# A two-layer token mixer on eight cores: pooling as running sums on VectorE with one grouped projection, a reordered opening, a wide value projection and a new pacing of background work

## The chip, the cores and the metric

The program runs on the 8 cores of one Trainium2 chip; each core takes one sequence of the batch of 8. The time is the device time of the slowest core, in microseconds (us), and a kernel's figure is the median of its runs. A core's *span* is the time from its first to its last instruction, and the *granted clock* is the share of TensorE's full speed that the hardware allows it at that time. Cores 0 to 3 are one die of the chip, 4 to 7 the other. A run can fall into a slower state, in which some cores show a lower granted clock than the others. Only runs outside that state are compared here, unless it is said.

Names in the profile: PE is TensorE, PEld its weight loads, DVE is VectorE, ACT is ScalarE, POOL is GpSimd, SP is SyncE. "ps" is a PSUM bank (the memory that TensorE writes its results to; all other tiles named here lie in SBUF, the main memory on the core), H the normalised input of a sub-layer, ACTB the SwiGLU products, X the residual stream, SLOTS the weights, WMOD the modulation rows, CB the conditioning vector (and later a pooling buffer), SQ and SP the squares and their pair sums (this SP is a tile and not the engine), RS the reciprocal root mean squares, TP temporaries, PMH the pooling input. All operations are issued through one helper, so every line carries the same number (L323 before, L331 after); they are told apart by tiles.

## The reference, cut to what matters

```python
for l in range(2):
    mod_f1, mod_mx, mod_f2 = split(silu(c) @ w_mod[l] + b_mod[l], 3)   # shift, scale, gate each
    x = x + 0.5 * gate * swiglu(modulate(x, mod_f1), w_ffn_in[l, 0], w_ffn_out[l, 0])
    x = x + gate * (mixer_ab(h) if l % 2 == 0 else mixer_pool(h))
    x = x + 0.5 * gate * swiglu(modulate(x, mod_f2), w_ffn_in[l, 1], w_ffn_out[l, 1])
return rmsnorm(x, final_g)
# modulate(x) = rmsnorm(x) * g * (1 + scale) + shift

def mixer_pool(h, w_grp, scale):            # layer 1 only
    cum = jnp.cumsum(h, axis=1)
    for i, w in enumerate((2, 4, 8, 16)):   # four groups of 256 channels
        prev = shift cum by w tokens
        p = (cum - prev) / minimum(t + 1, w) - h     # trailing mean minus the token itself
        outs.append(p @ w_grp[i])
    return concatenate(outs) * scale
```

The width is 1024, a sequence has 2048 tokens, and the SwiGLU's hidden width is 2816.

## The kernel before

The kernel keeps the 2048 tokens of a core as four tiles of 512 and treats them in two passes, p0 and p1, of two tiles. Each SwiGLU of each pass is a gate/up stage and a down stage for a first group of hidden columns, then the same for a second group. Everything that isn't a large matmul (the squares and sums for the next normalisation, the pooling, the modulation rows) is *background work*. The program is scheduled at build time: a generator yields steps, and after each segment of four to sixteen large matmuls `pump` may issue one.

```python
def pump(n=1, rows=True):
    for _ in range(n):
        if bg and bg_state[0] <= Sd.tl["pe"].tail():
            bg_step()                      # one step of the first generator in bg
    if rows:
        rows_pump()

def rows_pump():                           # ROW_EVERY = 7
    row_tick[0] += 1
    if row_tick[0] % ROW_EVERY == 0:
        ...                                # dot product of one modulation row, on VectorE

def square_pair(c, t):                     # one step of the statistics
    qs = [sq_rot.next(), sq_rot.next()]
    for i, q in enumerate(qs):
        act(SQ[:, q, :], Xv(c + i, t), AF.Square, ...)
    z = sp_rot.next()
    op = add("pool", I("tensor_tensor", out=SP[:, z, :], in0=SQ[:, qs[0], :], in1=SQ[:, qs[1], :], op=ALU.add), ...)
    return z, op.end + 0.3                 # summed over channels later by a matmul with ONES
```

The pooling is a background generator too. It projects first and applies the window afterwards, as a product with a banded 128x128 matrix. TensorE does both (cut):

```python
def pm_gen(p):
    for i in range(4):                                     # window w = 2 ** (i + 1)
        ... # VectorE and ScalarE: PMH = modulated input of two channel chunks, two tiles
        for n2 in range(4):                                # projection, 256 columns
            for k in range(2):
                for kc in range(2):
                    mm(PS[bk][:, k * 256:(k + 1) * 256], PMH[...tokens...], PMW[...], ..., n=256)
            act(GTv[...], PS[bk][:], AF.Copy, ...)
        for dd in range(2):
            for tt in range(2):
                for n in range(4):                         # band, 128 columns
                    mm(PS[bk][:, n * 128:(n + 1) * 128], GTv[...], BANDv[i], ..., n=128)
                    mm(PS[bk][:, n * 128:(n + 1) * 128], prev, BPREVv[i], ..., n=128)
                stt(Xv(dch, t), PS[bk][:], GH[...], Xv(dch, t), ALU.mult, ALU.add, ...)
```

It runs beside the second half of layer 1's first SwiGLU for p0, and beside the first pass of its second SwiGLU for p1. I call these two stretches (down of group 0, then gate/up of group 1) the *pooling windows*.

Two more parts matter. The opening loads x first, then the modulation rows. And at three boundaries between stages the reciprocal root of the statistics (Ln and Exp on ScalarE) is put ahead of the last gate/up segments (the prediction calls it rstd):

```python
side = build_h(nxt) if last and nxt is not None else iter(())
if last and late_norm:
    rstd(other, after=Sd.tl["pe"].tail())
run_segs([first[0], tail3[0], tail3[1], first[1], tail3[2], first[2]], side)
```

## Time and profile before

| | before |
|---|---|
| time | 2031.86 us, median of 4 runs (2030.88 to 2032.13) |
| profiled run, cores 0, 1, 4 to 7 | spans of 2027.4 to 2030.1 us, mean granted clock 0.979 to 0.995 |
| profiled run, cores 2 and 3 | 2057.0 and 2055.4 us, clock 0.965 and 0.966 |

In the profiled run, cores 2 and 3 were disturbed. So I read the other cores, mostly core 5. The page itself is of the slowest core, 2. These are its line of busy times and the first line of its chain of work that ended last.

```profile
PE 1994.9 (97%) x9458; PEld 934.6 (45%) x9458; DVE 1463.5 (71%) x2848; ACT 928.2 (45%) x1523; POOL 328.9 (16%) x431
...
PE 90%; DVE 5%; ACT 2%; DMA 1%; POOL 1%; issue 0%; SPq 0%; DVEq 0%; POOLq 0%
```

TensorE is busy for 97% of the span and makes up 90% of the chain. The list of TensorE's waits on core 5, from 62 us to the end, has the columns total, number and longest; these are its main lines.

```profile
PE ps L323 <- DVE ACTB L323: 9.6, 4, 3.0
PE ps L323 <- POOL SP L323: 3.6, 2, 2.7
PE ps L323 <- DVE X L323: 3.1, 3, 1.4
PE ps L323 <- DVE ps L323: 2.7, 5, 0.9
```

Three of the four waits on ACTB, 2.9 to 3.0 us each, are the three boundaries shown in code above. In the timeline one of them is the bracket at the end of this line (start, duration, then the wait of 3.01 us before it):

```profile
1535.52 14.81 PE L323 MATMUL ps<-ACTB,SLOTS 128*128 128x512 f16 x62 [3.01 <-DVE ACTB L323]
```

The groups of TensorE that belong to the value projection (first line) and to the pooling (the other two: projection, then band) are these, on core 5: count, busy time, mean ns, and idle time before them.

```profile
L323 PE MATMUL ps<-SLOTS,H 128*128 128x256 f16 x256 | 30.6, 273 | 0.0
L323 PE MATMUL ps<-WMOD 128*128 128x256 f16 x128 | 19.2, 273 | 0.0
L323 PE MATMUL ps<-PMC,WMOD 128*128 128x128 f16 x240 | 19.1, 219 | 0.0
```

The busy time overlaps between pipelined matmuls, so it overstates: the 256-column ones last 273 ns each but start 109 ns apart. What a matmul delays the next is read from the starts: 0.2153 us for 512 columns (0.2158 in the mean of all dense stretches of core 5). VectorE was idle for 19 us in the opening, waiting for the first modulation row (list of VectorE's waits, 0 to 80 us):

```profile
DVE ACTB L323 <- DMA ACTB<-wmod: 18.9, 1, 18.9
```

For the comparison I cut each core's trace at fixed counts of weight matmuls. That gives a ledger: the duration of each stage, the sum of TensorE's waits in it, and its *work* (columns / 2400 + 0.0026 us per matmul, a fit to the starts of dense matmuls in before: 0.2158, 0.1092 and 0.0558 us apart for 512, 256 and 128 columns; it fits dense stretches within 0.1 us). What remains I call the *remainder*. On core 5 of before it is 26.0 us. Of this, 16.5 us are the end of the program after the last matmul, some 5 us are three stretches of 3.41 us at a granted clock of 0.5 behind the boundary waits, and some 3 us lie in the first stage, which runs at 0.5 up to 67.0 us. The rest is gaps too short to count as waits.

### The profile page before, as it was taken

How to read it: one execution, taken by the hardware profiler on the slowest of the kernel's cores; microseconds unless marked ns; L12 is line 12 of the kernel's file. 1: busy time of each engine (PE TensorE's matmuls, PEld its weight loads, DVE VectorE, ACT ScalarE, POOL GpSimd, SP SyncE). 2: the span in 40 equal slices, each digit the busy share in tenths (PEclk: the TensorE clock that was granted, in tenths of full speed). 3: DMA queues.
4: the chain of work that ended last, by engine and by line, in shares of the span. 5: the costliest groups of instructions: out<-in, count | busy, mean ns of one | idle time of the engine just before them, and what ended most of it. 6: DMA issues, size and time to landing. Idle time of an engine off the chain costs nothing.

```text
span 2057.0 us, 26258 instructions; the slowest of 8 cores (2027.4 to 2057.0 us)
## 1 busy us (share of the span) xinstructions
PE 1994.9 (97%) x9458; PEld 934.6 (45%) x9458; DVE 1463.5 (71%) x2848; ACT 928.2 (45%) x1523; POOL 328.9 (16%) x431
## 2 busy tenths in 40 slices
PE   5899999999999899999999999999999999999996
PEld 4444444445454344444444444444544445444442
DVE  4876897777787967697779855865775547675654
ACT  4433644254353541554155524554673435744242
POOL 3102030014040200120002100110122001220001
PEclk5899999999999999999999999999998889999998
DMA  9795868675666566667766654445343442446652
GB/s 279 169 242 118 173 136 178 144 151 114 140 108 142 93 124 146 125 139 156 160 135 145 134 97 79 78 85 90 57 80 57 77 69 52 82 65 110 140 85 82
DMA packets 71390, 248.77 MB, mean 121 GB/s; under 512 B 7136, under 2 KB 7264, under 8 KB 70752
## 3 DMA queue, kind: packets, MB, share of 16 engines
q0 software_dynamic: 46928, 153.63, 45.9%
q1 hardware_dynamic: 24336, 93.45, 13.7%
q8 instruction: 79, 1.29, 0.2%
q14 instruction: 47, 0.39, 0.1%
HBM read 392.29 MB, written 8.39 MB: 195 GB/s over the span
## 4 chain that ended last, share of the span: by engine, by line
PE 90%; DVE 5%; ACT 2%; DMA 1%; POOL 1%; issue 0%; SPq 0%; DVEq 0%; POOLq 0%
PE ps L323 90%; DVE X L323 1%; DVE TP L323 1%; DVE SLOTS L323 1%; DMA WMOD<-wmod 1%; POOL SP L323 1%; DMA X<-xT 1%; DVE ACTB L323 1%; DVE H L323 1%; ACT H L323 1%; ACT L323 0%; DVE WMOD L323 0%; ACT RS L323 0%; POOL STAT L323 0%; DVE STAT L323 0%
## 5 line engine op out<-in xcount | busy, mean ns | idle before, releaser
L323 PE MATMUL ps<-H,SLOTS 128*128 128x512 f16 x5440 | 1226.3, 383 | 6.2 <-DVE ps L323 2.4
L323 PEld LDWEIGHTS ps<-H,SLOTS 128*128 128x128 f16 x5440 | 534.4, 99 | 652.6 <-issue 67.6
L323 PE MATMUL ps<-ACTB,SLOTS 128*128 128x512 f16 x3072 | 695.3, 386 | 12.0 <-DVE ACTB L323 8.9
L323 ACT ACTIVATE ps<-ps 128x512 f32<-128x512 f32 x528 | 307.2, 582 | 599.6 <-PE ps L323 586.2
L323 PEld LDWEIGHTS ps<-ACTB,SLOTS 128*128 128x128 f16 x3072 | 303.7, 99 | 384.1 <-issue 57.7
L323 DVE SCALAR_TENSOR_TENSOR X<-ps,GH,X 128x512 f32<-128x512 f32 x320 | 233.1, 747 | 151.0 <-PE ps L323 150.0
L323 DVE TENSOR_TENSOR ACTB<-TP,ps 128x512 f16<-128x512 f32 x368 | 251.5, 687 | 108.9 <-PE ps L323 71.4
L323 ACT ACTIVATE TP<-ps 128x512 f32<-128x512 f32 x400 | 238.7, 597 | 176.9 <-PE ps L323 174.5
L323 DVE TENSOR_TENSOR SLOTS<-SLOTS 128x512 f16<-128x512 f16 x704 | 310.2, 460 | 9.8 <-DMA SLOTS<-win 0.4
L323 DVE TENSOR_TENSOR TP<-ps,TP 128x512 f32<-128x512 f32 x176 | 121.6, 691 | 209.4 <-ACT ps L323 208.8
L323 POOL DMA_DIRECT2D SLOTS<-win x176 | 95.3, 541 | 1023.7 <-PE ps L323 997.3
L323 ACT ACTIVATE SQ<-X 128x512 f32<-128x512 f32 x224 | 134.3, 624 | 213.7 <-DVE X L323 142.5
L323 POOL TENSOR_TENSOR SP<-SQ 128x512 bf16<-128x512 f32 x112 | 153.3, 1373 | 195.7 <-ACT SQ L323 193.9
L323 DVE SCALAR_TENSOR_TENSOR WMOD<-WMOD,CB 128x512 f32<-128x512 f32 (+1 forms) x259 | 175.5, 708 | 3.2 <-DMA WMOD<-wmod 3.1
L323 DVE TENSOR_TENSOR ps<-ps,TP 128x512 f32<-128x512 f32 x176 | 122.9, 698 | 35.6 <-PE ps L323 35.3
L323 ACT ACTIVATE H<-TP,MODT,AS 128x512 f16<-128x512 f32 x160 | 121.3, 805 | 48.8 <-DVE TP L323 41.4
L323 DVE TENSOR_TENSOR TP<-X,RS 128x512 f32<-128x512 f32 x192 | 129.9, 714 | 6.3 <-ACT RS L323 3.9
L323 POOL DMA_DIRECT2D SLOTS<-wout x64 | 45.5, 710 | 336.3 <-PE ps L323 336.3
L323 PE MATMUL ps<-SP,ONES 128*128 128x512 bf16 x122 | 49.3, 416 | 26.4 <-POOL SP L323 22.2
L323 DVE TENSOR_TENSOR H<-H 128x1024 f16<-128x1024 f16 (+1 forms) x72 | 43.7, 628 | 2.9 <-ACT H L323 1.9
L323 ACT ACT_TABLE_LOAD x29 | 37.2, 1283 | 1.5 <-PEq L329 1.1
L323 POOL DMA_DIRECT2D SLOTS<-wab x28 | 15.9, 568 | 128.0 <-PE ps L323 127.6
(76 smaller groups left out, 493.9 us busy)
## 6 DMA issues: line engine op xcount, KB each, us to landing
SLOTS<-win POOLq DMA_DIRECT2D x176, 512.0 KB, 5.5
WMOD<-wmod SPq DMA_DIRECT2D x134, 512.0 KB, 6.1
SLOTS<-wout POOLq DMA_DIRECT2D x32, 768.0 KB, 8.8
SLOTS<-wout POOLq DMA_DIRECT2D x32, 640.0 KB, 6.9
SLOTS<-wab POOLq DMA_DIRECT2D x28, 512.0 KB, 7.5
X<-xT SPq DMA_DIRECT2D x4, 2048.0 KB, 17.3
outT<-X SPq DMA_DIRECT2D x16, 512.0 KB, 4.6
ACTB<-wmod SPq DMA_DIRECT2D x10, 512.0 KB, 19.9
```

The costliest lines, as they stand in the source:

```text
L323: return lambda E: getattr(E, name)(*a, **k)
```

## The change

The intent is to take work off the bounding engine. The window sum of pooling becomes a running sum over tokens on VectorE (add the token that enters, subtract the one that leaves), and TensorE only multiplies the result by the grouped weights, in 512-column matmuls. The extra VectorE work is to be spread by a pacing that looks at how far VectorE is behind in the build-time schedule. The statistics at the three boundaries are finished later, the opening loads modulation rows before x and shares them between TensorE and VectorE, and the value projection uses 512 columns. The diff, cut to its core:

```diff
+    def slack():
+        return Sd.tl["dve"].busy_after(Sd.tl["pe"].tail() - 0.5) < SLACK      # SLACK = 2.0 us
+
     def pump(n=1, rows=True):
-        for _ in range(n):
-            if bg and bg_state[0] <= Sd.tl["pe"].tail():
+        for _ in range(2 * n):
+            if bg and bg_state[0] <= Sd.tl["pe"].tail() and slack():
                 bg_step()
@@ rows_pump
-        if row_tick[0] % ROW_EVERY == 0:
+        if row_tick[0] >= ROW_EVERY and slack():
+            row_tick[0] -= ROW_EVERY
@@ v_stats: one 512-column matmul per channel chunk, was two of 256
@@ pm_gen (the band matrices of pm_consts and the projection of 256 columns are gone)
+   add("dve", I("tensor_tensor_scan", sv, PMH[:, c, cols], PMH[:, c, 16 - w + tt * TT:16 - w + (tt + 1) * TT],
+                init, ALU.add, ALU.subtract), ...)
+   add("dve", I("tensor_copy", SLAST[:, ch:ch + 1], PMS[:, (tt + 1) * TT - 1:(tt + 1) * TT]), ...)
+   op = stt(out, PMH[:, c, cols], -float(w), sv, ALU.mult, ALU.add, ...)   # w = 2: one subtraction instead
...
+                    for kc in range(2):
+                        mm(PS[bk][:], PMW[...], PMD[:, kc, tt * TT:(tt + 1) * TT], kc == 0, kc == 1, ...)
@@ opening
-    x loaded ahead of nine rows; squares in pairs; each chunk's shift row on PE, scale row on VectorE
+    six rows loaded, then x, then three rows; nine of the sixteen rows on PE; squares straight to bf16 in SP
@@ phase loop
-                if last and late_norm:
-                    rstd(other, after=Sd.tl["pe"].tail())
-                run_segs([first[0], ...], side)
+                late = last and late_norm
+                run_segs([first[0], ...], iter(()) if late else side)
+                if late:
+                    rstd(other, after=Sd.tl["act"].tail())
```

## The prediction

> **What bounds the kernel now.** TensorE. The page gives PE 97% of the span and 90% of the chain that ended last. On undisturbed core 0 (2027.4 us) the list of waits gives PE only about 23 us of waits after 60 us. The timeline shows dense 512-column matmuls at 0.2153 us each, so only PE columns, PE waits and the opening can pay. VectorE is busy 71%, but more where the background work runs.
>
> **Pooling, PE side (gain, certain).** Timeline of core 0, 1410-1500 and 1650-1730 us: a projection bank (4 matmuls of 256) delays PE by 0.44 us, a band bank (8 of 128) by 0.445. Removed: 128 x 0.109 + 248 x 0.056 = 27.8 us. Added: 64 matmuls of 512 x 0.2153 = 13.8 us. Net -14 us.
>
> **Pooling, VectorE side (cost).** Added per pass: 12 scans, 12 multiply-adds (about 0.73 us), 4 fp16 subtractions (0.42). [...] In the windows where it must fit (1412.6-1517 and 1643.5-1748 us) VectorE is busy 75 and 72 us of 104.4. [...] the statistics that follow (before: 1501-1512 us, paced by GpSimd) must still end before the drain. I expect PE waits of about 5 us per pass (0 to 12), +10 us together.
>
> **Late rstd.** Three boundaries (250, 1534, 1765 us) each have a 3.0 us PE wait on the SwiGLU product, because ScalarE runs Ln/Exp and its table loads ahead of the gate evacuations. Deferring it removes 9 us, but the next h is then built in about 28 us of down projection that already hold about 30 us of VectorE work. Net -4 us.
>
> **Opening.** Steady matmuls start at 61.9 us. VectorE idles 19 us waiting for the first modulation row behind x, then limits: 4.5 to 4.9 us busy per 5 us from 40 to 65 us. Three of its eight rows (1.5 us each) move into that idle time, one moves to PE, and about 2.5 us of pooling-constant work leaves. Against it, x lands some 10 us later (3.1 MB at about 315 GB/s). From my sum, first sustained matmuls at 55-58 us: -5 us.
>
> **Value projection.** 16 x 256 columns take 1.75 us per block, 8 x 512 should take 1.73: -0.3 us. Weight loads halve, but they are hidden. Pacing of rows by VectorE backlog: -1 us.
>
> **Sum:** -14 + 10 - 4 - 5 - 1 = about -14 us; allowing for what I may have missed, 2018 us. Range 2003 to 2034. Faster by over 2%: 0.03; within 2%: 0.95; slower by over 2%: 0.02.
>
> **What would show each step.** Pooling PE: no 256- or 128-column pooling matmuls, 64 of 512, PE busy down by some 14 us. VectorE: [...] VectorE over 90% in the two pooling windows, and new PE waits on VectorE or GpSimd near their ends; if they are under 1 us, my cost is wrong. Late rstd: the 3.0 us waits gone, with new waits on X or ps just after. Opening: VectorE's 19 us wait gone, sustained matmuls by 58 us. Value: same time per block.
>
> **What would make it wrong.** [...] If the drains serialise VectorE, PE, ScalarE and GpSimd, both passes lose over 10 us and the gain vanishes. If row loads and casting weight loads collide in the opening, its gain turns negative.

For matmuls see the starts above. Weight loads of 99 ns overlap them: from 60 to 1900 us of core 0 PE is busy 1818 us and PEld 847. Ahead of boundary 2 on core 5, ScalarE runs a table load (1.28 us), Ln and Exp (1.33 and 1.13) from 1523.0 us and another table load (1.28) at 1530.4; VectorE waits 1.70 us for the evacuation behind that, and TensorE 3.01 us for VectorE's product. In the opening the DMA moved 272 to 354 GB/s on core 0 (10 to 35 us).

## The result

| | before | after |
|---|---|---|
| median (range), 4 runs each, same chip | 2031.86 (2030.88 to 2032.13) | 2040.84 (2037.8 to 2041.15) |
| ratio of fast runs | 1 | 1.0042, 95% interval 1.0024 to 1.0059 |
| profiled cores, undisturbed | 2027.4 to 2030.1 | 2031.8 to 2035.5 |

A ratio is the mean time of one kernel's fast runs over that of the other's fast runs of the same rounds, so it is not quite the ratio of the medians. The change is within 2%, but it made the kernel 0.4% slower, and the time lies above the predicted range of 2003 to 2034. All runs are correct.

The page of after (its slowest core, 0), busy line and chain:

```profile
PE 1964.4 (97%) x9042; PEld 897.8 (44%) x9042; DVE 1513.6 (74%) x2874; ACT 911.8 (45%) x1503; POOL 313.4 (15%) x410
...
PE 80%; DVE 15%; DMA 2%; ACT 1%; issue 1%; POOL 0%; SPq 0%; DVEq 0%; POOLq 0%
```

VectorE's share of the chain rose from 5% to 15%. TensorE lost the work it was meant to lose. These are the groups of core 5 that replace those shown of before:

```profile
L331 PE MATMUL ps<-SLOTS,H 128*128 128x512 f16 x128 | 28.3, 379 | 0.0
L331 PE MATMUL ps<-CB,WMOD 128*128 128x512 f16 x64 | 18.2, 379 | 0.0
```

The ledger of core 5 gives TensorE's work as 1919.7 us before and 1905.3 after: 14.4 us less. But its waits grew from 22.3 to 37.7 us, and the remainder from 26.0 to 29.2. The list of waits of core 5 tells which kind grew:

```profile
PE ps L331 <- DVE ps L331: 19.9, 14, 2.9
PE ps L331 <- DVE X L331: 7.7, 7, 1.7
PE ps L331 <- POOL SP L331: 4.9, 4, 2.7
...
PE ps L331 <- DVE ACTB L331: 0.8, 1, 0.8
```

The 3.0 us waits on ACTB are gone; one of 0.8 us is left. Waits for GpSimd (SP) grew little. In their place come 14 waits for VectorE operations in PSUM ("DVE ps") of up to 2.9 us, and 7 on X. Where they lie, from the ledger (median over the undisturbed cores):

| stage (us) | before | after |
|---|---|---|
| opening + first gate/up | 58.94 + 78.21 | 59.36 + 75.52 |
| boundary 1, down | 38.70 | 36.33 |
| gate/up after it | 75.12 | 77.16 |
| layer 0, SwiGLU 2, first gate/up of p0 and of p1 | 77.43 and 76.32 | 78.49 and 77.35 |
| layer 1, SwiGLU 1, p0: first gate/up | 74.25 | 79.76 |
| pooling window 1 (down + gate/up) | 44.86 + 72.42 | 44.03 + 73.85 |
| boundary 2, down; gate/up after it | 39.34; 74.25 | 35.71; 76.78 |
| pooling window 2 (down + gate/up) | 44.97 + 72.76 | 44.03 + 72.54 |
| boundary 3, down; gate/up after it | 39.38; 74.25 | 34.78; 80.55 |

The pooling windows came out even. They took 235.0 us before and 234.5 after, although TensorE has 14 us less to do in them: it waits 6.0 and 4.9 us there, and 1.2 to 1.3 us more in each are remainder. That is short gaps around the waits, not a lower clock: the granted clock is 1.00. This is the gate/up stage of window 1 on core 5, before and after. The columns are window, length, then busy time and count for PE, PEld, DVE, ACT and POOL, then granted clock, DMA share and GB/s.

```profile
1454.10:1526.50 72.40, 72.40 (x427) 37.93 (x426) 50.73 (x90) 52.44 (x91) 15.45 (x17) 1.00 0.45 76
```

```profile
1456.30:1530.10 73.80, 67.76 (x309) 29.48 (x308) 63.67 (x113) 41.36 (x75) 14.95 (x17) 1.00 0.45 74
```

VectorE's busy time rose by 12.9 us and TensorE, no longer full, stands for 6 us. Over the whole window VectorE is busy 100.4 of 117.9 us, or 85%; in window 2, 84%. The groups of VectorE that are new, on core 5:

```profile
L331 DVE TENSOR_TENSOR_SCAN WMOD<-PMH,SLAST 128x512 f32<-128x512 f16 x18 | 24.2, 1345 | 0.0
...
L331 DVE SCALAR_TENSOR_TENSOR CB<-PMH,WMOD 128x512 f16<-128x512 f16 x24 | 17.2, 716 | 0.1
...
L331 DVE TENSOR_TENSOR_SCAN WMOD<-PMH 128x512 f32<-128x512 f16 x6 | 7.3, 1215 | 0.0
...
L331 DVE COPY SLAST<-WMOD 128x1 f32<-128x1 f32 x24 | 3.7, 153 | 0.8
```

Those four sum to 52.4 us.

But the pooling windows don't explain the loss. The opening and its first stage gained 2.3 us. The three boundaries gained too, but with the gate/up stages after them they came out even (341.0 and 341.3 us). What lost is the gate/up stages, and the largest new loss outside a boundary, 5.5 us, is the first gate/up stage of layer 1: no pooling runs there, and no statistic is deferred into it. Here is its start. In the timeline of core 5 before (start, duration, engine, operation, count):

```profile
1126.94 2.28 DVE L323 TENSOR_TENSOR SLOTS<-SLOTS 128x512 f16<-128x512 f16 x3
...
1127.41 2.95 POOL L323 TENSOR_TENSOR SP<-SQ 128x512 bf16<-128x512 f32 x2
...
1128.23 1.03 PE L323 MATMUL ps<-H,SLOTS 128*128 128x512 f16 x4
```

And after:

```profile
1123.64 2.97 DVE L331 SCALAR_TENSOR_TENSOR AS<-MODT,SM 128x8 f32<-128x8 f32 x1
...
1124.08 2.50 POOL L331 TENSOR_TENSOR SP<-SQ 128x512 bf16<-128x512 f32 x2
...
1127.10 1.27 POOL L331 TENSOR_TENSOR SP<-SQ 128x512 bf16<-128x512 f32 x1 [0.52 <-ACT SQ L331]
1127.20 1.73 DVE L331 SCALAR_TENSOR_TENSOR WMOD<-WMOD,CB 128x512 f32<-128x512 f32 x1
...
1128.65 1.40 POOL L331 TENSOR_TENSOR SP<-SQ 128x512 bf16<-128x512 f32 x1 [0.27 <-ACT SQ L331]
...
1128.85 1.74 DVE L331 SCALAR_TENSOR_TENSOR WMOD<-WMOD,CB 128x512 f32<-128x512 f32 x1
...
1131.36 1.02 PE L331 MATMUL ps<-H,SLOTS 128*128 128x512 f16 x4 [2.92 <-DVE ps L331]
```

A scalar-tensor product over 8 columns (AS) took 2.97 us, while two additions of GpSimd, 2.50 us together, ran. Two row products of 512 columns took 1.73 and 1.74 us (0.68 before), each over one more addition of GpSimd. Behind them stood the addition in PSUM that TensorE waited for: 2.92 us. After the wait TensorE's granted clock fell, as the next stretch of the same core shows (the clock is the 0.63 near the end of the line):

```profile
1131.30:1135.30 4.00, 3.94 (x12) 1.54 (x13) 3.77 (x11) 1.16 (x2) 0.00 (x0) 0.63 0.77 209
```

So the waits of 2.92 and 0.32 us cost 5.5 us of the stage: 3.2 us themselves and 2.2 us of remainder. Some 1.7 us of the latter are the clock: its record shows 0.5 for 3.41 us from 1132.37 us on, and the 512-column matmuls in that stretch follow each other at 0.427 us in place of 0.2153.

### The profile page after: what moved, and what is told of

Same layout as the page of the kernel before. It is cut to its first block, busy times and chain, and to the rows that moved or that the text cites. A ratio compares the mean times of both kernels' runs of the same rounds, so it can differ in the third digit from the quotient of the medians.

```text
span 2035.5 us, 25423 instructions; the slowest of 8 cores (2031.8 to 2035.5 us)
## 1 busy us (share of the span) xinstructions
PE 1964.4 (97%) x9042; PEld 897.8 (44%) x9042; DVE 1513.6 (74%) x2874; ACT 911.8 (45%) x1503; POOL 313.4 (15%) x410
## 4 chain that ended last, share of the span: by engine, by line
PE 80%; DVE 15%; DMA 2%; ACT 1%; issue 1%; POOL 0%; SPq 0%; DVEq 0%; POOLq 0%
PE ps L331 80%; DVE X L331 4%; DVE TP L331 3%; DVE SLOTS L331 2%; DVE WMOD L331 2%; DVE H L331 2%; DMA WMOD<-wmod 2%; DVE ACTB L331 1%; DMA SLOTS<-win 1%; DVE ps L331 0%; DVE CB L331 0%; ACT H L331 0%; ACT ps L331 0%; ACT PMH L331 0%; POOL SP L331 0%
## 5 line engine op out<-in xcount | busy, mean ns | idle before, releaser
L331 PE MATMUL ps<-H,SLOTS 128*128 128x512 f16 x5440 | 1209.6, 381 | 30.1 <-DVE ps L331 19.7
L331 PE MATMUL ps<-ACTB,SLOTS 128*128 128x512 f16 x3072 | 676.6, 379 | 3.0 <-DVE X L331 3.0
L331 ACT ACTIVATE SQ<-X 128x512 f32<-128x512 f32 x208 | 124.1, 624 | 156.6 <-DVE X L331 106.3
L331 DVE SCALAR_TENSOR_TENSOR WMOD<-WMOD,CB 128x512 f32<-128x512 f32 (+1 forms) x258 | 186.0, 752 | 3.4 <-DMA WMOD<-wmod 3.3
L331 POOL TENSOR_TENSOR SP<-SQ 128x512 bf16<-128x512 f32 x104 | 141.8, 1370 | 164.6 <-ACT SQ L331 156.1
L331 DVE TENSOR_TENSOR TP<-X,RS 128x512 f32<-128x512 f32 x192 | 130.3, 709 | 12.9 <-ACT RS L331 11.8
L331 ACT ACTIVATE PMH<-TP,MODT,AS 128x512 f16<-128x512 f32 x32 | 25.6, 810 | 43.9 <-DVE TP L331 43.8
## 6 DMA issues: line engine op xcount, KB each, us to landing
ACTB<-wmod SPq DMA_DIRECT2D x10, 512.0 KB, 22.3
```

Of the source, the lines that this page charges most:

```text
L331: return lambda E: getattr(E, name)(*a, **k)
```

## The experiments

My first theory, held right after the result, was that the *row pacing* bunches the modulation rows at the heads of gate/up stages (theory 1). Its rivals were that deferring the statistics moved more VectorE work into the next stage than it saved, that the new pooling costs more than it saves, and that the pacing of the *other* background work is to blame. Labels that begin with a_ are kernels derived from after, those with b_ or c_ from before; "_2" is a repetition. Spans are compared between the median undisturbed cores of one profiled run each.

### Row pacing undone

```diff
-        if row_tick[0] >= ROW_EVERY and slack():
-            row_tick[0] -= ROW_EVERY
+        if row_tick[0] % ROW_EVERY == 0:
```

> The changed kernel with only the pacing of the modulation rows put back (a row at every 7th step, no test of VectorE's backlog). Theory 1 (the new pacing delays rows until they are forced out in a burst at the head of a half): the first gate/up stage of layer 1, 79.8 us after the change against 74.25 before, falls back to about 74.3, the two of layer 0's second SwiGLU lose about 1 us each, and the time falls by 5 to 9 us to about 2033. Rival (the longer stage comes from the deferred rstd or from the pooling, not from the rows): under 2 us.

Only one of six runs was fast, at 2040.54 us. The profiled run had die 0 undisturbed: the first gate/up stage of layer 1 fell from 79.76 only to 77.67 us, and the span grew by 1.8 us. Theory 1 fell.

### Deferred statistics undone

```diff
-                run_segs([first[0], ...], iter(()) if late else side)
-                if late:
-                    rstd(other, after=Sd.tl["act"].tail())
+                if last and late_norm:
+                    rstd(other, after=Sd.tl["pe"].tail())
+                run_segs([first[0], ...], side)
```

> The changed kernel with only the deferral of Ln/Exp at three boundaries put back. Theory 1 (it only moves the wait: three 3 us waits go, but the next gate/up stage waits for an h that VectorE finishes too late): the three down stages grow by about 3 to 4 us each, the three gate/up stages after them shrink by 2.5 to 6 us each, sum within 3 us of the changed kernel. Rival (the deferral is a real gain that something else eats): 8 to 10 us slower than the changed kernel, about 2049.

Median 2044.54 us (2043.56 to 2046.61). The ratio of 1.0007 (0.990 to 1.011) is unclear, because one of before's fast runs was a disturbed 2056. In the ledger the three boundary stages grow by 4.7, 5.4 and 6.3 us, and the gate/up stages after them shrink by 0.3, 2.3 and 6.0; the span grows by 5.8 us. So the deferral gains some 4 to 8 us in this kernel (by time, span and stages), after giving back about half. It isn't the loss.

### New pooling undone

```diff
-    (running sums, PMH with a halo, 512-column projection)
+    (pm_consts, pm_load and pm_gen of the kernel before, with its band matrices)
```

> The changed kernel with the old pooling (band matrices on TensorE) put back, everything else as changed. Theory 1 (TensorE's 14 us saved come back as waits on a full VectorE): within 3 us of the changed kernel, the two gate/up stages with pooling at 72.4 us with under 1 us of PE waits in place of 6.0 and 4.9. Rival (the pooling's gain is mostly kept and the loss lies elsewhere): 8 to 14 us slower than the changed kernel.

Fast runs of 2035.77, 2036.72 and 2038.43 us; the ratio of 0.9969 (0.982 to 1.012) is unclear for the same reason. The span is 2.2 us shorter than after's. Inside the changed kernel the new pooling gains nothing.

### New opening undone

```diff
-    (rows, x, rows; stats0, row0)
+    (the opening of the kernel before: x, then rows)
```

> The changed kernel with only the old opening put back. Theory 1 (the new opening gains what the ledger of the two traces shows): 3 to 5 us slower than the changed kernel, about 2045, all of it before 140 us. Rival (the shorter opening only moves later work of VectorE or of the weight loads): within 1.5 us.

Fast runs of 2045.83, 2047.57 and 2048.51 us (ratio 1.0023, unclear), span 8.7 us longer. The new opening gains 5 to 9 us here, more than the 2.3 us that opening and first stage show directly: without it two later stages, the second gate/up (66.53 against 61.30 us) and the next pass's first (80.27 against 77.16 in the ledger), grow as well.

### Pacing, alone and undone, on a throttled chip

Each part but the pacing had turned out too small to be the loss, by spans and by unclear ratios. The second call went to the pacing: undone in the kernel after, and put alone into the kernel before.

```diff
# a_pump_old, from after:                        # b_pump, from before: the reverse, with slack(); rows as before
-        for _ in range(2 * n):
-            if bg and bg_state[0] <= Sd.tl["pe"].tail() and slack():
+        for _ in range(n):
+            if bg and bg_state[0] <= Sd.tl["pe"].tail():
```

> The changed kernel with only the pacing of the background work (statistics and pooling) put back: one step per segment and no backlog test, in place of up to two. Theory 2 (two statistics steps per segment put GpSimd's pair additions back to back at the head of the gate/up stages[...]): the first gate/up stage of layer 1 falls from 79.8 us to 74.3 to 76.5, the others of the later layers fall too, 8 to 15 us off the changed kernel's 2041, unless the pooling windows give up to 4 us of it back. Rival (the forced row bursts or the deferral make these waits): under 3 us.

> The kernel before with only the new pacing of background work (up to two steps per segment, under a test of VectorE's backlog); rows, rstd, opening, pooling and value projection as before. Theory 2: the first gate/up stage of layer 1 grows from 74.25 us to 77 to 80, in all 6 to 15 us slower than before. Rival (the pacing only hurts together with the new pooling or rows): within 3 us of before.

> The kernel before with the new opening, the wide value projection and the deferred rstd, but the old pooling and both old pacings. Theory 2 (these three parts gain, the pacing loses): 2014 to 2025, faster than both kernels; the first gate/up stage of layer 1 stays at 74.3 us. Rival (a shorter opening or the deferral always comes back as later waits): 2029 to 2036.

> The changed kernel with GpSimd's 104 pair additions taken away: ScalarE squares straight to bf16 and TensorE adds eight squares per tile in place of four pair sums (about 104 more matmuls, 22 us more of TensorE work). Theory 2[...]: the time by which VectorE's instructions exceed their own median, 58 us in the changed kernel, falls under 15 us, the first gate/up stage of layer 1 has under 0.5 us of PE waits in place of 3.2, and the time is only 4 to 12 us over the changed kernel's although 22 us of work are added. Rival (VectorE is simply late because too many rows and sums are queued): waits stay, 20 us or more slower.

What the theory rests on is the timelines above: VectorE operations are longer while GpSimd adds, 2.97 us for 8 columns in after, and 2.28 us for three additions of weights in before.

This chip was throttled as a whole: before itself took 2263.62 us there, at mean clocks of 0.87 to 0.92. All four kernels (2268.69, 2285.34, 2259.08 and 2267.34 us) are slow runs.

### The pacing alone, again

> The same kernel as b_pump (before, with only the new pacing of background work), again because that chip ran throttled. Theory 2: the first gate/up stage of layer 1 grows from 74.25 us to 77 to 80; 6 to 15 us slower than before. Rival: within 3 us of before.

2046.43 us (2045.31 to 2048.34) against 2032.86 for before on the same chip, ratio 1.0073 (1.0053 to 1.0093). **The new pacing of background work, with the rows left as they were, costs 14 us by itself.** With the old pooling, the old opening and the old boundaries, the ledger shows the same stage at the start of layer 1 longer (78.37 against 74.25 us), the gate/up of layer 0's SwiGLU 2 in p1 longer (80.46 against 76.32) and boundary 1 longer (43.17 against 38.70). The timeline of core 5 at the start of layer 1:

```profile
1136.58 6.56 DVE L331 TENSOR_TENSOR SLOTS<-SLOTS 128x512 f16<-128x512 f16 x4
...
1137.02 2.51 POOL L331 TENSOR_TENSOR SP<-SQ 128x512 bf16<-128x512 f32 x2
...
1140.05 1.36 POOL L331 TENSOR_TENSOR SP<-SQ 128x512 bf16<-128x512 f32 x1 [0.52 <-ACT SQ L331]
...
1141.60 1.26 POOL L331 TENSOR_TENSOR SP<-SQ 128x512 bf16<-128x512 f32 x1 [0.18 <-ACT SQ L331]
...
1143.89 1.01 PE L331 MATMUL ps<-H,SLOTS 128*128 128x512 f16 x2 [2.98 <-DVE ps L331]
```

Four additions of weights, each 0.42 us elsewhere, took 6.56 us together, over four additions of GpSimd. (One of the four took 3.24 us, over two of GpSimd's; one, between two of them, took 0.43.) The wait is 2.98 us. The gate/up of layer 0's SwiGLU 2 in p1 shows the same picture: four additions took 6.11 us, and TensorE then waited 2.98 us.

Boundary 1 is another case. Its longest wait on core 5 is this one, in place of one of 2.89 us before:

```profile
253.82 1.44 PE L331 MATMUL ps<-ACTB,SLOTS 128*128 128x512 f16 x3 [4.70 <-DVE ACTB L331]
```

No addition of GpSimd runs in the 9 us before it, and no VectorE operation there is overlong; the product that TensorE waits for only stands behind more row products and normalisations. So these 4.5 us of the 14 have a cause that isn't GpSimd, and no run isolates it. In the kernel after this boundary doesn't lose (36.33 us), since its statistics are deferred.

### The GpSimd additions taken away

If it is GpSimd's additions that hold VectorE up, then the changed kernel without them should lose these waits although TensorE gets more to do: ScalarE writes each square as bf16 and TensorE sums all eight instead of four pair sums.

```diff
-        for i, q in enumerate(qs):
-            act(SQ[:, q, :], Xv(c + i, t), AF.Square, ...)
-        op = add("pool", I("tensor_tensor", out=SP[:, z, :], in0=SQ[...], in1=SQ[...], op=ALU.add), ...)
+        z = (sp_rot.next(), sp_rot.next())
+        for i in range(2):
+            op = act(SP[:, z[i], :], Xv(c + i, t), AF.Square, ...)      # ones_mm is called for both
```

> The same kernel as a_nogp (the changed kernel without GpSimd's pair additions), again because that chip ran throttled; there VectorE's overlong time had fallen to 0.0 us. Theory 2: 0 us again, under 1 us of PE waits in the first gate/up stage of layer 1 in place of 3.2, in all 4 to 12 us over the changed kernel's 2041 with 22 us of TensorE work added. Rival: 20 us or more slower.

Correct; its fast runs are 2024.06 and 2025.08 us (four others were slow), ratio 0.9964 (0.994 to 0.9988): faster than both kernels, with 104 more matmuls (22.5 us more work of TensorE in the ledger). I had expected 4 to 12 us over the changed kernel, and it came out some 16 below: TensorE's waits fell to 11.7 us on core 5, below those of before (22.3) too. The schedule is built anew for it, so more than GpSimd's work changed; but the first gate/up of layer 1 takes 75.97 us, just its longer work, with no wait. The profiled run had die 1 undisturbed. The same place on core 5:

```profile
1121.39 0.53 POOL L331 DMA_DIRECT2D SLOTS<-win  x1 [9.83 <-PE ps L331]
...
1124.57 1.89 PE L331 MATMUL ps<-H,SLOTS 128*128 128x512 f16 x8
...
1125.73 1.21 DVE L331 TENSOR_TENSOR SLOTS<-SLOTS 128x512 f16<-128x512 f16 x3
```

GpSimd only issues a DMA there, no VectorE operation is longer than its kind, and TensorE doesn't stop. To put a number on it I summed, over all VectorE operations, the time by which each exceeds the median of its own form, where that is over 0.2 us:

| overlong VectorE time, core 5 | us |
|---|---|
| before | 48.9 |
| after | 57.9 |
| pacing alone | 52.2 |
| after without GpSimd's additions | 0.0 |

All of it is in operations without a PSUM operand. So VectorE was held up before as well, by 49 us, in places where TensorE seldom waited for it. With the new pacing the total grew by only 3 to 9 us. What costs is its place: in the stages shown, several VectorE operations in a row are held just ahead of one that TensorE needs. The amount alone tells little: c_double, below, has 59.4 us of it and is the fastest kernel here. The backlog test can't see it, because the schedule's cost model gives each operation its undisturbed time.

Each of these overlong operations on core 5 (61 in before and 58 in after, of the forms that occur at least five times) overlaps an addition of GpSimd in time. Another 79 and 71 without a PSUM operand overlap one and are not stretched by over 0.2 us. Of those with a PSUM operand, 94 and 71 overlap one, and none exceeds its median by over 0.01 us. What in the hardware makes this difference the traces don't show.

### Everything but the new pooling and pacing; then with the new pooling

```diff
# c_oldpool_2: before + new opening, 512-wide V, deferred statistics
# c_newpool:   c_oldpool_2 + new pooling; two steps per segment and slack() only while a pooling pass is in bg
+        for i in range(2 * n):
+            if bg and bg_state[0] <= Sd.tl["pe"].tail() and (slack() if pooling else i < n):
```

> The same kernel as c_oldpool (before, plus new opening, wide value projection and deferred rstd), again because that chip ran throttled all the time. Theory 2: 2014 to 2025, faster than both kernels; first gate/up stage of layer 1 about 74.3 us, PE waits after 62 us under 15 us in all. Rival: 2029 to 2036.

> c_oldpool with the new pooling, and the new pacing of background work only while a pooling pass and the statistics behind it are under way. Theory 2 (new pooling saves TensorE 14 us and gives as much back as waits, whatever the rest does): within 4 us of c_oldpool on the same chip, 4 to 6 us of PE waits in each pooling window. Rival (the pooling was only spoilt by the rest of the change): 8 to 14 us faster than c_oldpool, about 2006.

On one chip, with before at 2028.84: the first took 2025.26 us (median of four, one of them slow; fast runs 2023.1 to 2026.24; ratio 0.998, 0.9962 to 0.9997), the second 2022.9, 2022.92 and 2024.45, and once 2050.67 with cores 6 and 7 disturbed, which makes its ratio of 1.0017 inconclusive (0.9935 to 1.0099). So opening, value projection and deferral gain about 4 us of time (the median core's span fell by 8.6 us, from 2028.1 to 2019.5, but the slowest core's in that profile only to 2024.3); the new pooling adds about 1 us to that, which is no more than the scatter. The first gate/up of layer 1 is back at 74.25 us in both: confining the pacing to the pooling removed that loss. The pooling windows of the second are those of after, with waits of 6.06 and 4.86 us.

c_newpool differs from after in the pacing alone: the new one of background work is confined to the pooling passes, and the rows keep the old one. So it says most about the loss. It is 5.9 us below before on its chip (median of its three undisturbed runs), where after is 9.0 above on its own: the pacing outside the pooling costs the changed kernel about 15 us.

The parts now add up. Four gained, one gained, and 14 lost by the pacing make a loss of 9 us; after is 9.0 us above before. (By the spans of median cores it is 8.6 gained, 0.7 lost and 14.0 lost, a loss of 6.1; after is 6.6 above.) That it closes so well is partly luck: the runs are from several chips, and 4.5 of the 14 us lie at boundary 1, where after doesn't lose.

### What limits the pooling windows

The mechanism was open for the pooling windows: is it GpSimd there too, or VectorE's own added work? Three kernels, each derived from c_newpool or after:

```diff
# c_noscan: the scans and the copies of their last column left out, PMS set once (a wrong result on purpose)
-    add("dve", I("tensor_tensor_scan", sv, ...)); add("dve", I("tensor_copy", SLAST[...], ...))
# c_newpool_nogp: the squares to bf16 of a_nogp_2, only while a pooling pass and its statistics run
# a_pump_old_2: the kernel after with the old one-step pump everywhere
```

> c_newpool with the 24 scans and their 24 copies of the last column taken away (the multiply-add reads zeros; the result is wrong on purpose). Theory A (the waits in the two pooling windows are VectorE's load, of which the scans are about 15 us per pass): the waits of 6.1 and 4.9 us there fall under 1 us each, the two windows (down plus gate/up) shrink from 117.9 and 116.6 us to about 111, and the time is 10 to 13 us under c_newpool's 2023.7. Rival B (the waits come from the order of the steps or from GpSimd's adds alone): they stay over 3 us each.

> c_newpool with only the statistics behind the two pooling passes squared without GpSimd's adds (16 more matmuls, 3.4 us of TensorE work). Theory A (load decides[...]): waits fall from 6.1 and 4.9 us to about 4 and 2.5 us, as in the changed kernel without any of GpSimd's adds, the windows to about 117.3 and 115; 1 to 3 us under c_newpool. Rival B[...]: they vanish, 7 us under c_newpool.

(Theory A leaves a small part of the waits to GpSimd's additions, and rival B gives them all of it.)

> The same kernel as a_pump_old (the changed kernel with only the pacing of background work put back), again because that chip ran throttled; there its two pooling gate/up stages took 86.1 and 84.4 us where the other three kernels of that call took 73 to 78. Expected on an undisturbed die: first gate/up stage of layer 1 at 74.3 to 77 in place of 79.8, the two pooling gate/up stages at 78 to 84 in place of 73.9 and 72.5: the pacing that the new pooling needs is what the statistics can't bear; in all within 6 us of the changed kernel.

Before took 2029.75 us on this chip. Without scans: fast undisturbed runs of 2012.76 and 2014.44 us (relative error 0.12; the other two runs were disturbed, 2038.28 and 2360.92); the two windows take 224.4 us against 234.5, and the waits fall from 6.06 and 4.86 to 1.36 and 1.27 us. Gate/up of window 1:

```profile
1448.80:1517.10 68.30, 66.94 (x309) 29.87 (x308) 51.85 (x85) 39.27 (x70) 14.96 (x17) 1.00 0.54 80
```

Without GpSimd's additions: 2023.17 and 2023.52 us (two further runs of 2048.8 and 2048.74 with a pair of cores disturbed). The span is 1.1 us below c_newpool's, on another chip, and the waits fall only to 3.98 and 2.84 us. So in the windows it is VectorE's own added work, the scans above all; GpSimd is a minor part.

With the old pump the changed kernel took 2065.89 us (2064.49 to 2066 in three runs, one of 2090.33; ratio 1.0207, 1.0151 to 1.0263). The one-step pump makes the pooling wait longer, 10.2 and 8.4 us, but that is not most of the loss of 36 us. Core 5 of it, from late in the first window on:

```profile
1489.00:1649.00 160.00, 154.80 (x588) 63.97 (x589) 105.71 (x175) 74.90 (x126) 27.88 (x31) 0.81 0.39 66
```

For some 160 us the granted clock was 0.81. On cores 0, 1 and 4 to 7 this began at about 1503 us, inside the first pooling window, on cores 2 and 3 at 1737 us, inside the second; each core lost about 30 us to it (0.19 of 160). It is the same clock as that of the disturbed pair in the profile of before, core 2:

```profile
1550.00:1670.00 120.00, 120.00 (x459) 49.71 (x458) 60.50 (x108) 47.95 (x81) 17.50 (x22) 0.81 0.43 73
```

Before had it on one pair of cores in the profiled run; this kernel had it on all of them there. To judge by the times of cores, one pair escaped it in each of two other runs: these cores took 2030.9 and 2037.6, 2033.0 and 2036.4 us, about what the cores of after take (2030.6 to 2039.0). My expectation, within 6 us of the changed kernel, was missed by the size of this episode. On the cores that escaped it the old pump shows no gain either, since the longer waits of the pooling take back what the first gate/up stages gain (76.02 us in place of 79.76 in layer 1). That long stop-and-go of TensorE brings the episode about is a guess, which no run tests. What is shown is that the new pooling with the old pump is, by its times, worse than either kernel.

### A version without scans

The scan is the costly piece, 1.215 us for 512 columns. A window sum of width 2, 4, 8 or 16 can be had by repeated doubling: add the array to itself shifted by 1, then by 2, 4, 8, in fp16 over both tiles at once.

```diff
+    sv, sk, d, z = PMH[:, c, :], hk, 1, 0
+    while d < w:
+        a = 16 - (w - 2 * d)
+        tt_(PAB[z][:, a:1040], sv[:, a:1040], sv[:, a - d:1040 - d], ALU.add, ..., half=True)
+        sv, sk, d, z = PAB[z], [("PAB", z)], 2 * d, 1 - z
+        yield
+    # then PAB[z] = -w * PMH by tensor_scalar, and PMD = PAB[z] + sv by tt_
-    (scan, copy of the last column, multiply-add)
```

> c_newpool with the window sums by doubling (s2 = h + h one token back, s4 = s2 + s2 two back, and so on: 1, 2, 3 fp16 additions of 1024 columns more per window size) in place of the scans, and a scale plus an addition in place of the multiply-add. Estimate from durations in the traces (0.63 us for a 1024-column fp16 addition, 1.27 us per scan, 0.72 us per multiply-add): about 7 us less VectorE work per pass. Theory A (VectorE's load makes the waits; 16 us less per pass gave 10 us back in c_noscan): waits of 6.1 and 4.9 us fall to 2 to 4 us, 4 to 7 us under c_newpool, about 2017 to 2020 where before is 2029. Rival: within 1.5 us of c_newpool.

Correct; 2018.57 us (2017.62 to 2021.74, 5 fast runs) against 2031.66 for before on the same chip: **ratio 0.9939 (0.9924 to 0.9954), faster than both kernels.** Three of its groups on core 5; the additions of some 1024 columns of fp16 take 0.68 us where nothing stretches them (last line; the first group's mean is 0.92, which I put down to GpSimd's additions without having looked it up in this trace), the scaling 0.42:

```profile
L331 DVE TENSOR_TENSOR CB<-WMOD 128x1024 f16<-128x1024 f16 x12 | 11.0, 919 | 0.3
...
L331 DVE TENSOR_SCALAR WMOD<-PMH 128x1024 f16<-128x1024 f16 x12 | 5.1, 421 | 0.0
...
L331 DVE TENSOR_TENSOR WMOD<-PMH 128x1026 f16<-128x1026 f16 x4 | 2.7, 681 | 0.0
```

All of these operations sum to 43.7 us, against 52.4 for scans, copies and multiply-adds. The gate/up of window 1 takes 68.5 us in place of 73.8, and TensorE's waits there fall to 1.6 us (in window 2 from 4.9 to 2.8, and 70.7 us in place of 72.5):

```profile
1451.80:1520.30 68.50, 66.87 (x310) 29.82 (x309) 59.09 (x107) 41.59 (x74) 15.21 (x17) 1.00 0.48 80
```

Over the run, its list of TensorE's waits has no "DVE ps" over 1.2 us any more; one of 2.9 us on X, at a boundary, is left:

```profile
PE ps L331 <- DVE ps L331: 9.4, 14, 1.2
PE ps L331 <- DVE X L331: 8.2, 7, 2.9
```

## Why the prediction was wrong, point by point

**The failed step: "Pacing of rows by VectorE backlog: -1 us".** I took the pacing for a change of the rows alone. For the rows the term was about right: undoing their pacing cost 1.8 us of span (a_rows_old). But the diff doubles the steps of *all* background work, and my sum had no term for that. It costs +14 us when put into before (b_pump_2), and about 15 us in the changed kernel (after against c_newpool). The squares and GpSimd's additions now come four in a row at the head of a gate/up stage. There VectorE's operations take longer (6.56 us for four additions of 0.42 us beside four of GpSimd, in b_pump_2); TensorE then waits about 3 us, and on six of the eight cores of after it runs at a granted clock of 0.5 for 3.4 or 6.8 us after it. This is shown for two stages, which make some 8 of the 14 us; the 4.5 us of boundary 1 have another cause, which stays open. That it is the doubling, and not the backlog test beside it, was not tested apart. With the measured +14 in place of -1 my sum gives about 2033 us. The other 8 us are in two terms: pooling gave 1 us in place of 4, and opening, value projection and late rstd together gave 4 us of time in place of 9.

- *Pooling, TensorE side: -14 us.* Right. The ledger's work fell by 14.4 us in all.
- *Pooling, VectorE side: +10 us of waits.* Right in size: 6.0 and 4.9 us, but partly by luck. I did not count 2.5 us of short gaps around the waits. Nor was I right about where: VectorE was busy 85% and 84% of the windows, not over 90%, and in window 1 the waits lie at 1470 to 1508 us of 1456 to 1530, not near the end. Netted, pooling is worth about 1 us where I had 4.
- *The scan.* It takes 1.215 us where undisturbed, and a 512-column addition 0.68 to 0.70 us in the same trace.
- *Late rstd: -4 us.* Right within the spread of the measurements, without the new pacing. The 3.0 us waits are gone, and waits on X and ps in the following stage give part of it back. The three boundaries with the stages after them take 341.0 us in before, 338.0 in c_oldpool_2 (a gain of 3.0) and 341.3 in after; undoing the deferral in after costs 5.8 us of span.
- *Opening: -5 us, sustained matmuls by 58 us.* Half right. On core 5 they start at 59.6 instead of 60.5 us, on the median core at 59.4 instead of 58.9, so that figure was missed; opening and first stage together gained 2.3 us directly, and undoing the opening cost 8.7. VectorE's 19 us wait is indeed gone. It became a wait for the statistics of x and a shorter one for rows:

```profile
DVE TP L331 <- ACT RS L331: 12.2, 1, 12.2
DVE ACTB L331 <- DMA ACTB<-wmod: 7.6, 3, 5.2
```

- *Value projection: -0.3 us.* Right to within reading: the first pass of that mixer went from 100.37 to 100.21 us.

The prediction's own warnings named the drains and the opening's loads. GpSimd stands there only as what paces the drains, not as an engine beside which VectorE's operations take longer. Yet the profile of before shows it: three additions of weights took 2.28 us beside GpSimd's pair (timeline above), where three take 1.21 us with GpSimd quiet (a_nogp_2).

**After a wait, the clock.** The granted clock fell to 0.5 after waits of TensorE of 3.01 us (before, core 5, at 1535 us) and 2.92 us (after, core 5; 0.63 over the 4 us shown above). No sharp limit shows. One wait of 2.38 us, at 1575 us in after, was not followed by a lower clock on core 5, but the same wait (2.37 us) was on core 0:

```profile
1576.90:1580.30 3.40, 3.40 (x10) 1.21 (x8) 1.78 (x3) 2.14 (x5) 1.27 (x1) 0.51 0.00 0
```

I counted the waits with no other near them on the undisturbed cores of twelve kept profiles. The clock fell to 0.5 after none of 564 waits of 0.8 to 1.5 us, 6 of 150 of 1.6 to 1.9 us, 44 of 102 of 2.3 to 2.7 us, and 96 of 118 of 2.9 to 3.0 us. (Counted again in before and after alone, on their undisturbed cores, between 75 and 1990 us: 0 of 79, 0 of 16, 9 of 24 and 20 of 26.) Each time it stayed there for 3.41 us, or twice that, which costs 1.7 us or 3.4. So a wait near 3 us mostly costs about 5 us.

**What stays open.** The parts interact, so no exact share can be given to each: undoing the opening in the changed kernel costs 8.7 us of span, but opening, value projection and deferral together gain only 4 us of time over before (8.6 us of the median core's span). And why one kernel meets the clock of 0.81 in all its runs, on most of its cores, isn't settled. It isn't the usual clock of dense matmuls on eight cores: in the profile of after all eight have a mean of 0.980 to 0.992. In that of before, cores 2 and 3 had 0.81 for 160 us from 1545 us on, while cores 0 and 1 of the same die had 1.00.

## What to carry to other kernels

A pacing rule at the level of the scheduler moves every kind of background work, so before costing it list each kind that it may move, and look up in a trace which engine's operations are longer beside it (here VectorE's, by 49 us in before, beside GpSimd's additions). When work moves from TensorE to an engine that is 70 to 85% busy, ask for its cheapest form there first: here the same window sums as fp16 doubling instead of scans turned an even trade into a gain. And a wait of 2.3 to 3 us on TensorE may cost 1.7 us more than itself (here after 140 of 220); look at the granted clock just after it.
